# A DiT backbone's first modulation: 16 chunks row-major on TensorE, in four strips of the array's columns

## The chip, the core and the metric

The kernel runs as one program on one core of a Trainium2 chip. The metric is the device time of one execution in microseconds (us). Engines are named as the profile names them: PE is TensorE (PEld its weight loads), DVE is VectorE, ACT is ScalarE, POOL is GpSimd, SP is the engine that issues the DMAs.

## The reference

Two interleaved layers over 256 latent and 256 context tokens of width 1024: a macaron pair of SwiGLU FFNs (width 2816) around a gated short convolution (layer 0) or a latent attention (layer 1). Every sub-layer is normed and modulated by shift, scale and gate, which are linear maps of SiLU(c) for the latents and SiLU(c_ctx) for the context:

```python
def adaln_chunks(cond, w_mod, b_mod):
    m = jax.nn.silu(cond) @ w_mod + b_mod
    return jnp.split(m[:, None, :], N_MOD, axis=-1)

def pre(h, g, shift, scale):
    return rms_norm(h, g) * (1 + scale) + shift

def swiglu(h, w1, w3, w2):
    return (jax.nn.silu(h @ w1) * (h @ w3)) @ w2
...
        h_x = h_x + 0.5 * mx[2] * ffn1(pre(h_x, g_norm[i, 0], mx[0], mx[1]))
```

The first thing that the network needs is therefore `mx[0]`, `mx[1]` and their context twins for layer 0: shift (j = 0) and scale (j = 1), each of 1024 features, that is 8 chunks of 128 features each, 16 chunks in all.

## The kernel before

Activations are kept feature-major: `h` is 8 chunks of 128 features by 512 tokens (latents 0 to 255, context 256 to 511). Products are made in three matmuls (`mm3`, L167 to L169): weights and activations are split into a high part rounded to fp32r and a low rest, and high x high, low x high and high x low are added up in PSUM. Weights come as "units" of up to 128 x 2048 fp32 (1 MB), one DMA each into one of two `raw` buffers; `conv_unit` (L144, L145) makes the high part `wh` on ACT and the low part `wl` on DVE, in three buffers. A unit of the FFN's first product holds 8 blocks for w1 and 8 for w3, one block of 128 columns for each of the 8 contraction chunks.

The modulation is 144 chunks of 128 x 1024 (512 KB). `mod_order` sets their order; the first 16 are shift and scale of the first norm, taken in turn (shift 0, scale 0, shift 1, ...). Nearly all are stored transposed: a feature in each partition, and DVE multiplies them by the two condition rows `crow` and sums along the free axis (`mod_step`, L243, tile `junk`), two products a chunk; with `share`, the second product of a scale chunk goes to GpSimd (`pj`, L239) and ACT sums it (L240). Three of the first 16 are stored row-major (`_by_rows`): TensorE multiplies them by the 2 conditions as stationary columns (L226), ACT copies the 2 x 128 result (L230, tile `row`), TensorE transposes it (L232) and DVE adds the bias (L233). The finished values are in `fin`.

The opening, up to the end of the first three units of the first FFN, is written out as a list of steps, `FIRST_ORDER`, which `run` in `build` goes through: m and M compute one modulation chunk (M with `share`), w issues a chunk's DMA, r a unit's, U converts a unit, C0 to C7 is `chunk(k)`: the normed and modulated chunk k of the activations (`nt` on DVE or GpSimd, `nu` in two halves on ACT, `yh` on ACT, `yl` on DVE), S starts the FFN, T takes the third unit, A0 to A7 are the products of contraction chunk k with the first two units (12 matmuls), B0 to B7 those with the third (6). Z ends the time in which DMAs are issued by the list alone. A scheduler then places the instructions of each engine in order; each engine runs its own in that order. All weight and modulation DMAs are issued by SP, in order too. The first chunks' tiles lie in the FFN's still unused buffers `gh` and `gl` (`early`), the others in four buffers `wm`.

After the opening, the background modulation is paced by `bg`, some two to three chunks a step.

Of the kernel before, what the change touches and what calls it, by code (L numbers as in the profile page):

```python
# [9 lines left out]
F32 = mybir.dt.float32  # L10
F32R = mybir.dt.float32r
AF = mybir.ActivationFunctionType
ALU = mybir.AluOpType
AX = mybir.AxisListType

P = 128
D = 1024
ND = D // P
NLAT = 256
NCTX = 256  # L20
T = NLAT + NCTX
# [14 lines left out]
KR_N = KV_LORA + QK_ROPE  # L36
FIRST_ORDER = """m w w m C0 m U M U S M r A0 C1 w w m w M M w w U T B0 C2 A1 w m C3 M w m B1 B2 A2 B3 w M A3 C4 M B4 r C5 w A4 w M Z m C6 A5 B5 M A6 B6 C7 A7 r B7"""
MLA_ORDER = """L0 Q01 Q00 Q02 L1 R N0 n0 n1 T1 Q12 T0 Q10 n2 n3 Q11 N1 X1 n4 n5 D0 n6 n7 D1 D2 D3 D4 D5 D6 O0 D7 U K00 L2 L3 K10 T2 T3 V0 X3 K20 K30 O1 V1 V2 V3 H K31 K21 K11 K01"""
# [9 lines left out]
V_BMOD = 0  # L48
V_GN = V_BMOD + DEPTH * NMOD * ND
# [11 lines left out]
MODB = 4  # L61
EARLY = ("gh", "gl", None, "gh")
MOD_US = 8.0
WCOLS = 16 * P
# [4 lines left out]
class Kern:  # L69
# [17 lines left out]

    # ---------------------------------------------------------------- weights
    def plan(self):
# [69 lines left out]

    # ---------------------------------------------------------------- products  # L160
    def mm3(self, ps, c, u, b, x, k, start, stop):
# [20 lines left out]

    # ---------------------------------------------------------------- modulation
    def mod_setup(self):
        nc = self.nc
        self.mod = self.const.tile([P, DEPTH, NMOD * ND, 2], F32, name="mod")
        self.fin = self.const.tile([P, DEPTH, NMOD * ND, 2], F32, name="fin")
        self.mod_order = []
        for l in range(DEPTH):
            for js in ((0, 1), (2,), (3, 4), (5,), (6, 7), (8,)):  # L190
                for c in range(ND):
                    for j in js:
                        self.mod_order.append((l, j, c))
        self.mod_pos = 0
        self.mod_dma = 0
        self.mod_tiles = {}
        self.credit = 0.0
# [13 lines left out]

    def mod_step(self, share=False):
        if self.mod_pos >= len(self.mod_order):
            return
        nc = self.nc
        i = self.mod_pos
        self.mod_pos += 1
        l, j, c = self.mod_order[i]
        m = j * ND + c
        b = self.vec[:, V_BMOD + l * NMOD * ND + m:V_BMOD + l * NMOD * ND + m + 1]  # L220
        self.mod_dma_to(i + 1)
        w = self.mod_tiles.pop(i)
        if _by_rows(l, j, c):
            pr = self.mmps()
            for k in range(ND):
                nc.tensor.matmul(  # L226
                    pr[0:2, 0:P], self.cT[:, k, :], w[:, k * P:(k + 1) * P], start=k == 0, stop=k == ND - 1
                )
            row = self.gp.tile([2, P], F32, tag="row", name=self.nm("row"), bufs=2)
            nc.scalar.copy(row, pr[0:2, 0:P])  # L230
            pc = self.mmps()
            nc.tensor.transpose(pc[:, 0:2], row, self.ident[0:2, 0:2])  # L232
            nc.vector.tensor_scalar(self.fin[:, l, m, :], pc[:, 0:2], b, None, ALU.add)  # L233
            return
        for cond in range(2):
            o = self.mod[:, l, m, cond:cond + 1]
            if share and cond == 1 and j == 1:
                t = self.gp.tile([P, D], F32, tag="pj", name=self.nm("pj"), bufs=1)
                nc.gpsimd.tensor_tensor(t, w, self.crow[:, cond, :], ALU.mult)  # L239
                nc.scalar.activation(t, t, AF.Copy, accum_out=o)  # L240
                continue
            junk = self.gp.tile([P, D], F32, tag="junk", name=self.nm("junk"), bufs=1)
            ins = nc.vector.tensor_tensor_reduce(  # L243
                junk, w, self.crow[:, cond, :], 1.0, 0.0, ALU.mult, ALU.add, o
            )
            if share is False:
                self.tc.keep_in_program_order(ins)
        if not self.hold:
            self.mod_dma_to(i + 1 + MODB)
        src, dst = self.mod[:, l, m, :], self.fin[:, l, m, :]  # L250
        if j in (1, 4, 7):
            g = V_GN + (l * 3 + j // 3) * ND + c
            nc.vector.tensor_scalar(dst, src, b, 1.0, ALU.add, ALU.add)
            nc.vector.tensor_scalar(dst, dst, self.vec[:, g:g + 1], None, ALU.mult)
        elif j in (2, 8):
            nc.vector.tensor_scalar(dst, src, b, 0.5, ALU.add, ALU.mult)
        else:
            nc.vector.tensor_scalar(dst, src, b, None, ALU.add)  # L258

    def mod_need(self, l, js):  # L260
        need = max(i for i, (a, j, c) in enumerate(self.mod_order) if a == l and j in js)
        while self.mod_pos <= need:
            self.mod_step()
# [4 lines left out]
    def bg(self, us, quiet=False):  # L268
        """background modulation work, paced by the tensor engine's time"""
        self.credit += us  # L270
        n = 0
        while self.credit >= MOD_US and not quiet and n < 3:
            self.credit -= MOD_US
            self.mod_step()
            n += 1

    # ---------------------------------------------------------------- norms
    def rsqrt(self, ss, n, w, out):
# [63 lines left out]

    # ---------------------------------------------------------------- sublayer ends
    def residual(self, ps, d, c, l, j):
# [8 lines left out]
    def out_pair(self, u, x, ks, l, j, nxt, ctx_on):  # L353
        """last two chunks of a sub-layer's output, latents first, and the next norm"""
        nk = len(ks)
# [25 lines left out]
    def in_first(self, lat, ctx):  # L381
        """first groups of a sub-layer, contraction outermost, latents before the context"""
        for k in range(ND):
            for f in lat:
                f(k)
            if k == 1 and self.pending is not None:
                self.pending()
                self.pending = None
        for k in range(ND):
            for f in ctx:  # L390
                f(k)
# [3 lines left out]

    # ---------------------------------------------------------------- FFN
    def ffn_epi(self, p1, p3, g, f, w):
# [7 lines left out]
    def first_early(self, un, pss, g, l, j0):  # L405
        """first groups on unnormalized latents; the norm's factor is applied to their results"""
        nc = self.nc
# [100 lines left out]

    # ---------------------------------------------------------------- gated short convolution
    def conv_epi(self, pc, pu, pb, z, ch):  # L510
# [61 lines left out]

    # ---------------------------------------------------------------- latent attention
    def rot(self, src, tt, tabs, out, nh):
        """rotary halves of nh heads, token-major; gains are in the tables"""
        nc = self.nc
# [44 lines left out]
    def mla(self, l, nxt, mp):  # L621
        nc = self.nc
# [19 lines left out]

        # the rest of the last sub-layer's context; down projections, token-major
        held, g, ks, jg, sq = self.late
# [109 lines left out]

        # queries
        qps, qst = {}, {}
# [47 lines left out]

        # keys and values
        rctx = self.tmp.tile([P, T], F32, tag="rstd", name=self.nm("rstd"))[:, :NCTX]
# [85 lines left out]
        vv = []  # L892
        # heads, two at a time
        hp = QK_ROPE
# [106 lines left out]

    # ---------------------------------------------------------------- all
    def build(self):
# [19 lines left out]
        with self.tc.tile_pool(name="gp", bufs=1) as gp:  # L1023
            self.gp = gp
            self.mod_setup()
            for i in range(4):
                nc.sync.dma_start(self.h[:, 2 * i:2 * i + 2, :], a["hT"][:, 2 * i:2 * i + 2, :])
            self.mod_dma_to(2)
            self.dma_to(2)
            self.mod_dma_to(4)  # L1030
            self.crow = gp.tile([P, 2, D], F32, name="crow")
            nc.scalar.activation(self.cT, self.cT, AF.Silu)
            self.new_y()
# [36 lines left out]
            def run(ops, groups=None, more=None):  # L1070
                for op in ops:
                    k = int(op[1:] or 0)
                    if op[0] == "w":
                        self.mod_dma_to(self.mod_dma + 1)
                    elif op[0] == "r":
                        self.dma_to(self.dma_pos + 1)
                    elif op[0] == "M":
                        self.mod_step(True)
                    elif op[0] == "m":
                        self.mod_step(None)  # L1080
                    elif op[0] == "U":
# [34 lines left out]
def _by_rows(l, j, c):  # L1116
    """chunks of w_mod sent row-major, whose products go to the tensor engine"""
    return l == 0 and j == 0 and c < 3

# [86 lines left out]
```

## Time and profile before

| | |
|---|---|
| device time, median of 3 runs | 1659.9 us (1659.26 to 1659.95) |
| profiled execution: span, first to last instruction | 1657.4 us |
| what the runs' median has beside that span | 2.5 us |
| PE busy | 1614.2 us, 97% |
| DVE busy | 1156.7 us, 70% |
| ACT busy | 594.4 us, 36% |
| POOL busy | 94.3 us, 6% |
| DMA | 244.26 MB, mean 147 GB/s |
| granted TensorE clock, mean | 0.986 |

The profile has no separate device time of the profiled execution; its span stands in for it, and the runs' median is 2.5 us longer. A busy time is the time in which an engine has an instruction under way; matmuls overlap in it, so the distance between the starts of two matmuls, and not the duration of one, is what one costs. PEclk is the clock that the chip granted TensorE, as a share of full speed.

### The profile page before, as it was taken

How to read it: one execution, taken by the hardware profiler on the slowest of the kernel's cores; microseconds unless marked ns; L12 is line 12 of the kernel's file. 1: busy time of each engine (PE TensorE's matmuls, PEld its weight loads, DVE VectorE, ACT ScalarE, POOL GpSimd, SP SyncE). 2: the span in 40 equal slices, each digit the busy share in tenths (PEclk: the TensorE clock that was granted, in tenths of full speed). 3: DMA queues.
4: the chain of work that ended last, by engine and by line, in shares of the span. 5: the costliest groups of instructions: out<-in, count | busy, mean ns of one | idle time of the engine just before them, and what ended most of it. 6: DMA issues, size and time to landing. Idle time of an engine off the chain costs nothing.

```text
span 1657.4 us, 21462 instructions
## 1 busy us (share of the span) xinstructions
PE 1614.2 (97%) x8509; PEld 1380.1 (83%) x8509; DVE 1156.7 (70%) x2007; ACT 594.4 (36%) x936; POOL 94.3 (6%) x90
## 2 busy tenths in 40 slices
PE   6799999999999999999999999999999989999999
PEld 3588888888988898888888898888888976899999
DVE  7868667665897677766766677767664588786554
ACT  5342222323523253222232352222222466664442
POOL 3300000002000100000000200000000231010000
PEclk8899999999999999999999999999999979999999
DMA  7346445342254415444444425444432120146452
GB/s 306 135 148 221 154 140 195 141 157 102 81 212 170 172 52 194 162 165 152 167 164 165 140 77 186 157 162 156 165 140 102 58 77 1 67 163 216 167 202 102
DMA packets 46758, 244.26 MB, mean 147 GB/s; under 512 B 5313, under 2 KB 6593, under 8 KB 31041
## 3 DMA queue, kind: packets, MB, share of 16 engines
q1 hardware_dynamic: 46658, 242.90, 40.9%
q8 instruction: 66, 1.08, 0.3%
q14 instruction: 34, 0.28, 0.0%
HBM read 241.83 MB, written 1.05 MB: 147 GB/s over the span
## 4 chain that ended last, share of the span: by engine, by line
PE 90%; DVE 6%; DMA 2%; ACT 1%; issue 0%; POOL 0%; SPq 0%; DVEq 0%; ACTq 0%
PE mm L167 28%; PE mm L169 28%; PE mm L168 28%; DVE wl L145 1%; DVE junk L243 1%; DMA raw<-w 1%; DMA early<-wmod 1%; DVE yl L178 1%; PE mm L1045 0%; PE mm L942 0%; DVE nt L325 0%; PE mm L924 0%; PE mm L953 0%; DVE fin L258 0%; PE mm L687 0%
## 5 line engine op out<-in xcount | busy, mean ns | idle before, releaser
L167 PE MATMUL mm<-yh,wh 128*128 128x512 f32 (+1 forms) x1672 | 597.4, 358 | 6.2 <-ACT yh L177 4.1
L169 PE MATMUL mm<-yl,wh 128*128 128x512 f32 (+1 forms) x1672 | 595.3, 358 | 5.7 <-DVE yl L178 5.7
L168 PE MATMUL mm<-yh,wl 128*128 128x512 f32 (+1 forms) x1672 | 596.4, 357 | 0.8 <-DVE wl L145 0.8
L144 ACT CAST wh<-raw 128x1024 fp32r<-128x1024 f32 (+4 forms) x362 | 328.1, 931 | 618.6 <-PE mm L169 511.3
L145 DVE TENSOR_TENSOR wl<-raw,wh 128x1024 fp32r<-128x1024 f32 (+4 forms) x362 | 392.7, 1104 | 47.3 <-ACT wh L144 45.7
L167 PEld LDWEIGHTS mm<-yh,wh 128*128 128x128 f32 x1672 | 317.5, 190 | 53.1 <-ACT yh L177 4.9
L169 PEld LDWEIGHTS mm<-yl,wh 128*128 128x128 f32 x1672 | 317.0, 190 | 52.8 <-DVE yl L178 7.4
L168 PEld LDWEIGHTS mm<-yh,wl 128*128 128x128 f32 x1672 | 317.3, 190 | 46.2 <-DVE wl L145 1.5
L243 DVE CUSTOM_DVE_ANT_0 junk<-wm,crow 128x1024 f32<-128x1024 f32 x262 | 325.7, 1243 | 3.9
L167 PE MATMUL mm<-gh,wh 128*128 128x512 f32 (+1 forms) x848 | 294.9, 348 | 0.0
L169 PE MATMUL mm<-gl,wh 128*128 128x512 f32 (+1 forms) x848 | 294.4, 347 | 0.4 <-DVE gl L178 0.4
L168 PE MATMUL mm<-gh,wl 128*128 128x512 f32 (+1 forms) x848 | 294.2, 347 | 0.0
L402 DVE TENSOR_TENSOR s<-mm,s 128x512 f32<-128x512 f32 (+1 forms) x86 | 54.1, 629 | 246.7 <-PE mm L169 237.9
L169 PEld LDWEIGHTS mm<-gl,wh 128*128 128x128 f32 x848 | 160.5, 189 | 21.1 <-DVE gl L178 1.0
L349 DVE SCALAR_TENSOR_TENSOR h<-mm,fin,h 128x256 f32<-128x256 f32 x192 | 88.9, 479 | 127.7 <-PE mm L169 127.7
L168 PEld LDWEIGHTS mm<-gh,wl 128*128 128x128 f32 x848 | 160.5, 189 | 20.1
L167 PEld LDWEIGHTS mm<-gh,wh 128*128 128x128 f32 x848 | 160.5, 189 | 20.1
L401 ACT ACTIVATE s<-mm 128x512 f32<-128x512 f32 (+1 forms) x86 | 47.2, 548 | 193.4 <-PE mm L169 193.4
L178 DVE TENSOR_TENSOR gl<-s,gh 128x512 fp32r<-128x512 f32 (+1 forms) x86 | 53.5, 623 | 2.6 <-ACT gh L177 2.6
L297 POOL COPY acc<-sq 128x512 f32<-128x512 f32 (+1 forms) x5 | 4.4, 875 | 858.6 <-ACT sq L293 858.6
L293 ACT ACTIVATE sq<-h 128x256 f32<-128x256 f32 (+1 forms) x50 | 25.4, 508 | 72.9 <-DVE h L349 71.2
L177 ACT CAST gh<-s 128x512 fp32r<-128x512 f32 (+1 forms) x86 | 48.5, 564 | 4.4 <-DVE s L402 4.4
(187 smaller groups left out, 1064.0 us busy)
## 6 DMA issues: line engine op xcount, KB each, us to landing
raw<-w SPq DMA_DIRECT2D x104, 1024.0 KB, 4.8
wm<-wmod SPq DMA_DIRECT2D x132, 512.0 KB, 3.6
raw<-w SPq DMA_DIRECT2D x32, 896.0 KB, 4.5
raw<-cin_cu SPq DMA_DIRECT2D x8, 1024.0 KB, 4.9
early<-wmod SPq DMA_DIRECT2D x12, 512.0 KB, 10.4
raw<-cin_b SPq DMA_DIRECT2D x8, 512.0 KB, 3.8
raw<-cout SPq DMA_DIRECT2D x4, 1024.0 KB, 4.8
raw<-wo SPq DMA_DIRECT2D x4, 1024.0 KB, 4.8
```

The costliest lines, as they stand in the source:

```text
L144: self.nc.scalar.copy(h[:, b0:b1], raw[:, b0:b1])
L145: self.nc.vector.tensor_tensor(l[:, b0:b1], raw[:, b0:b1], h[:, b0:b1].bitcast(F32), ALU.subtract)
L167: mm(o, wh[:, b], xh[:, k, c[0]:c[1]], start=start, stop=False)
L168: mm(o, wl[:, b], xh[:, k, c[0]:c[1]], start=False, stop=False)
L169: mm(o, wh[:, b], xl[:, k, c[0]:c[1]], start=False, stop=stop)
L177: self.nc.scalar.copy(h, src)
L178: self.nc.vector.tensor_tensor(l, src, h.bitcast(F32), ALU.subtract)
L243: ins = nc.vector.tensor_tensor_reduce(junk, w, self.crow[:, cond, :], 1.0, 0.0, ALU.mult, ALU.add, o)
L293: nc.scalar.activation(sq[:, c[0]:c[1]], self.h[:, d, c[0]:c[1]], AF.Square)
L349: self.nc.vector.scalar_tensor_tensor(hh, ps[:, lo:hi], self.f(l, j, d, cond), hh, ALU.mult, ALU.add)
L401: nc.scalar.activation(s[:, :w], p1[:, :w], AF.Silu)
L402: nc.vector.tensor_tensor(s[:, :w], p3[:, :w], s[:, :w], ALU.mult)
```

## The change

All 16 chunks of the first modulation are now row-major (`_by_rows` is true for layer 0, j < 2), and `mod_rows` computes them in four groups G0 to G3 of four chunks: shift and scale of norm chunks 2g and 2g + 1. The conditions are padded with zeros to 32 columns (`cTp`). For each of 8 contraction chunks, four matmuls of 32 stationary columns on 128 moving ones go to four strips of 32 columns of the array, and their results to four strips of partitions of one PSUM tile. One copy of 128 x 128, one transpose and three DVE operations finish a group. `share` with its GpSimd and ACT path is gone, and `mod_pos` starts at 16. The list puts two norm chunks behind each group; four chunks of the second modulation (m) are done on DVE at the list's end. The DMAs of the first two groups are issued ahead: four chunks before the first two units, four behind them.

```diff
-FIRST_ORDER = """m w w m C0 m U M U S M r A0 C1 w w m w M M w w U T B0 C2 A1 w m C3 M w m B1 B2 A2 B3 w M A3 C4 M B4 r C5 w A4 w M Z m C6 A5 B5 M A6 B6 C7 A7 r B7"""
+FIRST_ORDER = """G0 U C0 C1 U S A0 A1 U T G1 C2 B0 B1 C3 A2 A3 B2 B3 G2 C4 A4 B4 C5 A5 B5 w w w w G3 Z C6 m A6 B6 C7 m A7 B7 m m"""
...
+NROW = 16
+CP = 32
...
-        self.mod_pos = 0
+        self.mod_pos = NROW
...
-        if _by_rows(l, j, c):
-            pr = self.mmps()
-            for k in range(ND):
-                nc.tensor.matmul(
-                    pr[0:2, 0:P], self.cT[:, k, :], w[:, k * P:(k + 1) * P], start=k == 0, stop=k == ND - 1
-                )
-            row = self.gp.tile([2, P], F32, tag="row", name=self.nm("row"), bufs=2)
-            nc.scalar.copy(row, pr[0:2, 0:P])
-            pc = self.mmps()
-            nc.tensor.transpose(pc[:, 0:2], row, self.ident[0:2, 0:2])
-            nc.vector.tensor_scalar(self.fin[:, l, m, :], pc[:, 0:2], b, None, ALU.add)
-            return
         for cond in range(2):
             o = self.mod[:, l, m, cond:cond + 1]
-            if share and cond == 1 and j == 1:
-                t = self.gp.tile([P, D], F32, tag="pj", name=self.nm("pj"), bufs=1)
-                nc.gpsimd.tensor_tensor(t, w, self.crow[:, cond, :], ALU.mult)
-                nc.scalar.activation(t, t, AF.Copy, accum_out=o)
-                continue
...
+    def mod_rows(self, g):
+
+        nc = self.nc
+        ws = [self.mod_tiles.pop(4 * g + q) for q in range(4)]
+        pr = self.mmps()
+        for k in range(ND):
+            for q, w in enumerate(ws):
+                nc.tensor.matmul(
+                    pr[q * CP:(q + 1) * CP, 0:P], self.cTp[:, k, :], w[:, k * P:(k + 1) * P],
+                    start=k == 0, stop=k == ND - 1, tile_position=(0, q * CP))
+        row = self.tmp.tile([P, T], F32, tag="t2", name=self.nm("row"), bufs=1)[:, 0:P]
+        nc.scalar.copy(row, pr[:, 0:P])
+        pc = self.mmps()
+        nc.tensor.transpose(pc[:, 0:P], row, self.ident)
+        src = pc[:, 0:P].rearrange("p (c j x) -> p c j x", c=2, j=2)
+        for j in range(2):
+            m = j * ND + 2 * g
+            v = lambda o: self.vec[:, o:o + 2].unsqueeze(2).broadcast_to([P, 2, 2])
+            dst = self.fin[:, 0, m:m + 2, :]
+            nc.vector.tensor_tensor(dst, src[:, :, j, 0:2], v(V_BMOD + m), ALU.add)
+            if j:
+                nc.vector.scalar_tensor_tensor(dst, dst, 1.0, v(V_GN + 2 * g), ALU.add, ALU.mult)
...
-            self.mod_dma_to(2)
+            self.mod_dma_to(4)
             self.dma_to(2)
-            self.mod_dma_to(4)
+            self.mod_dma_to(8)
             self.crow = gp.tile([P, 2, D], F32, name="crow")
-            nc.scalar.activation(self.cT, self.cT, AF.Silu)
+            self.cTp = gp.tile([P, ND, CP], F32, name="cTp")
+            nc.vector.memset(self.cTp, 0.0)
+            nc.scalar.activation(self.cTp[:, :, 0:2], self.cT, AF.Silu)
...
-                    if op[0] == "w":
+                    if op[0] == "G":
+                        if k < 2:
+                            self.dma_to(k + 3)
+                            self.mod_dma_to(4 * k + 12)
+                        self.mod_rows(k)
+                    elif op[0] == "w":
                         self.mod_dma_to(self.mod_dma + 1)
...
-                    elif op[0] == "M":
-                        self.mod_step(True)
...
-    return l == 0 and j == 0 and c < 3
+    return l == 0 and j < 2
```

How the scheduler places this shows at three places. First ScalarE, from the norm's factor on to the second unit's casts, before (`row` is the copy ahead of the transpose, `nu` a half of a norm chunk, `yh` its high part, `wh` a unit's high part):

```order
L230 COPY row_166<-mm_157 2x128
L144 CAST wh_201<-raw_99 128x512 x2
L1058 ACTIVATE nu_181<-nt_180,fin 128x256 x2
L144 CAST wh_218<-raw_101 128x512
L177 CAST yh_107<-nu_181 128x512
L144 CAST wh_218<-raw_101 128x512 x3
L230 COPY row_196<-mm_187 2x128
L240 ACTIVATE pj_213,mod<-pj_213 128x1024
```

and now:

```order
L255 COPY row_207<-mm_174 128x128
L1067 ACTIVATE nu_225<-nt_224,fin 128x256
L146 CAST wh_214<-raw_101 128x512 x4
L1067 ACTIVATE nu_225<-nt_224,fin 128x256
L1067 ACTIVATE nu_232<-nt_231,fin 128x256
L179 CAST yh_114<-nu_225 128x512
L1067 ACTIVATE nu_232<-nt_231,fin 128x256
L146 CAST wh_238<-raw_103 128x512
L179 CAST yh_114<-nu_232 128x512
```

The first unit's four casts and half of chunk 1 moved between the two halves of chunk 0 and its `yh`.

Second TensorE, around G1, now (`mm_253` is the last group of A1, `mm_297` the block's PSUM tile, `mm_288` the third unit's first group):

```order
L171 MATMUL mm_253<-yl_115,wh_238 128x512
L251 MATMUL mm_297<-early_105,cTp 32x128 x32
L257 MATMUL mm_332<-cst,row_330 128x128
L169 MATMUL mm_288<-yh_114,wh_278 128x512
L170 MATMUL mm_288<-yh_114,wl_279 128x512
L171 MATMUL mm_288<-yl_115,wh_278 128x512
```

Before, the three row-major chunks all stood ahead of the first product:

```order
L1047 MATMUL mm_109<-acc,ones 128x512
L226 MATMUL mm_157<-early_96,cT 2x128 x8
L232 MATMUL mm_168<-cst,row_166 128x2
L226 MATMUL mm_187<-early_96,cT 2x128 x8
L232 MATMUL mm_198<-cst,row_196 128x2
L226 MATMUL mm_234<-early_171,cT 2x128 x8
L232 MATMUL mm_245<-cst,row_243 128x2
L167 MATMUL mm_230<-yh_107,wh_201 128x512
```

Only G0 still does; G1 to G3 stand between products (three matmuls of G2 ahead of A2, its other 29 with all of G3 ahead of A4), the transposes of G1 and G2 directly behind their block, and that of G3 behind B5.

Third SP, the DMAs from the activations on, now (`early_96` is G0, `early_105` G1, `wm` of 166 to 172 G2, `early_292` G3, `raw` the units):

```order
L1034 DMA h<-hT 128x1024 x4
L210 DMA early_96<-wmod 128x1024 x4
L129 DMA raw_101<-w 128x2048
L129 DMA raw_103<-w 128x2048
L210 DMA early_105<-wmod 128x1024 x4
L129 DMA raw_164<-w 128x2048
L210 DMA wm_166<-wmod 128x1024
L210 DMA wm_168<-wmod 128x1024
L210 DMA wm_170<-wmod 128x1024
L210 DMA wm_172<-wmod 128x1024
L129 DMA raw_290<-w 128x2048
L210 DMA early_292<-wmod 128x1024 x4
```

Before, two chunks stood ahead of the first two units and four behind them; the third unit has G2 behind it now, and the fourth G3.

## Rows read from the trace of the kernel before

**Rows 1.** Page, part 2: the span in 40 slices of 41.4 us

```profile
PE   6799999999999999999999999999999989999999
...
PEclk8899999999999999999999999999999979999999
```

**Rows 2.** Windows: us, each engine's busy us (instructions), granted clock, DMA, GB/s

```profile
0.00:85.57 85.57, 59.48 (x205) 39.55 (x206) 69.49 (x99) 41.96 (x74) 29.44 (x20) 0.88 0.57 213
85.57:300.00 214.43, 214.43 (x947) 177.55 (x946) 152.12 (x249) 58.23 (x74) 0.00 (x0) 1.00 0.48 171
```

**Rows 3.** TensorE's waits up to 90 us: us, times, longest

```profile
PE mm L232 <- ACT row L230: 7.8, 3, 4.6
PE mm L169 <- DVE yl L178: 5.7, 3, 4.0
...
PE mm L167 <- ACT yh L177: 4.1, 2, 2.8
```

**Rows 4.** Timeline of TensorE: start, us, what, [idle before <-releaser]

```profile
16.63 2.82 PE L226 MATMUL mm<-early,cT 128*2 128x128 f32 x16
...
20.25 1.91 PE L226 MATMUL mm<-early,cT 128*2 128x128 f32 x16 [0.25 <-DMA early<-wmod]
...
25.13 3.40 PE L226 MATMUL mm<-early,cT 128*2 128x128 f32 x16
```

**Rows 5.** Timeline of ScalarE and VectorE, first norm chunk

```profile
19.48 0.25 ACT L230 COPY row<-mm 2x128 f32<-2x128 f32 x1 [0.31 <-PE mm L226]
...
20.25 0.21 DVE L233 TENSOR_SCALAR fin<-mm,vec 128x2 f32<-128x2 f32 x1
...
21.09 1.09 ACT L1058 ACTIVATE nu<-nt,fin 128x256 f32<-128x256 f32 x2 [0.32 <-DVE nt L1056]
...
22.60 0.61 ACT L177 CAST yh<-nu 128x512 fp32r<-128x512 f32 x1
...
34.16 2.17 ACT L144 CAST wh<-raw 128x512 fp32r<-128x512 f32 x4
```

**Rows 6.** Timeline of TensorE: pitch of its matmuls in the opening

```profile
33.34 0.80 PE L167 MATMUL mm<-yh,wh 128*128 128x512 f32 x1
...
38.63 0.80 PE L167 MATMUL mm<-yh,wh 128*128 128x512 f32 x2
...
75.66 0.50 PE L167 MATMUL mm<-yh,wh 128*128 128x512 f32 x1 [2.82 <-ACT yh L177]
...
80.11 0.39 PE L167 MATMUL mm<-yh,wh 128*128 128x512 f32 x1
...
85.57 0.39 PE L167 MATMUL mm<-yh,wh 128*128 128x512 f32 x1
```

**Rows 7.** Timeline of TensorE around a matmul on 64 rows, in the attention

```profile
1383.79 0.39 PE L923 MATMUL mm<-wh,arl 128*128 128x512 f32 x1
1384.11 0.50 PE L924 MATMUL mm<-wh,arh 64*128 64x512 f32 x1
1384.54 0.50 PE L922 MATMUL mm<-wl,arh 128*128 128x512 f32 x1
```

**Rows 8.** VectorE's and GpSimd's products up to 84 us; timeline at 36 us

```profile
L243 DVE CUSTOM_DVE_ANT_0 junk<-early,crow 128x1024 f32<-128x1024 f32 x14 | 19.2, 1374 | 0.0
...
L239 POOL TENSOR_TENSOR pj<-early,crow 128x1024 f32<-128x1024 f32 x4 | 11.4, 2860 | 0.4 <-ACT pj L240 0.4
...
35.91 2.82 POOL L239 TENSOR_TENSOR pj<-early,crow 128x1024 f32<-128x1024 f32 x1
...
36.42 2.34 DVE L253 TENSOR_SCALAR fin<-mod,vec 128x2 f32<-128x2 f32 x1
```

**Rows 9.** SP's issues; GB/s to 100 us, 40 slices of 2.5

```profile
10.19 1.94 SPq L208 DMA_DIRECT2D early<-wmod  x4
27.80 0.33 SPq L127 DMA_DIRECT2D raw<-w  x1
...
GB/s 6 224 379 367 408 428 426 410 398 48 0 79 410 418 419 411 426 380 359 48 0 41 216 162 16 210 324 288 0 0 0 0 0 0 7 216 256 367 69 298
```

More of the change, by code (lines that the diff above doesn't have):

```diff
@@ L210, in mod_dma_to, with mod_step @@
             self.mod_dma += 1
-    def mod_step(self, share=False):
+    def mod_step(self):
         if self.mod_pos >= len(self.mod_order):
@@ L245, in mod_step @@
             )
-            if share is False:
-                self.tc.keep_in_program_order(ins)
+            self.tc.keep_in_program_order(ins)
         if not self.hold:
@@ L1072, in run @@
                     k = int(op[1:] or 0)
-                    if op[0] == "w":
+                    if op[0] == "G":
[4 more added lines that the diff above has]
+                    elif op[0] == "w":
                         self.mod_dma_to(self.mod_dma + 1)
-                    elif op[0] == "r":
-                        self.dma_to(self.dma_pos + 1)
-                    elif op[0] == "M":
-                        self.mod_step(True)
                     elif op[0] == "m":
-                        self.mod_step(None)
+                        self.mod_step()
                     elif op[0] == "U":
```

## Prediction

> **What bounds the kernel now.** Read the page first: TensorE is busy in nine tenths or more of every slice but the first one or two and a few near the end, at full clock [rows 1]. So only a stretch where it waits can give time back. The windows place that stretch: up to 85.57 us TensorE is busy 59.48 us at a mean granted clock of 0.88, and from there to 300 us it is never idle [rows 2]. 85.57 us is where the fourth weight unit's first matmul starts. In this opening the 205 TensorE records are 8 for the condition rows, 2 for the norm's sum, 48 + 3 for the three row-major chunks and 144 for the three first weight units (8 contraction chunks, 6 groups, 3 products). At the pitch of the last 24, (85.57 - 80.11) / 24 = 0.2275 us [rows 6], the 144 need 32.8 us; they took 85.57 - 33.34 = 52.2. The opening's waits say for what: the transposed row (7.8 us), then yl and yh of the first norm [rows 3]. Behind these stand VectorE and GpSimd. VectorE's modulation products cost 19.2 us for 14 of its 20, GpSimd's 11.4 us for 4 of its 6; and while GpSimd multiplies (35.91 to 38.73), a VectorE fin of 128x2 elements lasts 2.34 us, where the like takes 0.21 [rows 8, 5]. So the reader should see a serial norm chain, held up by modulation work on two engines that stop each other. Order rows say that TensorE's sequence after the opening is the same in both kernels, so what is won or lost up to the fourth unit stays.
>
> **What the change takes away and adds.** It removes 20 VectorE products and 6 GpSimd ones for the first 16 chunks (20 x 1.37 = 27 and 6 x 2.86 = 17 us at the means of rows 8), which then no longer stand between the norm chunks. Four further chunks ("m", two products each) follow with the last norm chunks; I cost them at nothing, since they are taken from later work and VectorE is busy only 152 of 214 us after the opening [rows 2]; without that slack they would be 8 x 1.37, some 11 us. It adds four blocks G0 to G3 on TensorE, which did not exist: 32 matmuls each instead of 8, a copy of 128x128, a transpose and three small VectorE operations.
>
> *The price of a block.* Eight such matmuls with 2 stationary columns make 16 records, and took 2.82, 1.91 and 3.40 us [rows 4]: 1.91 at the clock's upper level (2.4 GHz; 0.119 us a record), 3.40 at the lower (1.2). No row shows four strips of columns at work together. If nothing overlaps a block is 4 x 1.91 = 7.6 us; if the four overlap fully, 1.9. I take 3.8, the middle that one mechanism gives: each matmul is two records in the same strip, which follow each other, and if starts stay in order only one record of a strip can run beside one of the next, so a block is 32 x 0.119 = 3.8. The Trainium skill, "TensorE: Matmul & The Clock Gate" (Part 3), has matmuls in strict order and a measured 2.38-fold gain for three column tiles; by that a block would be an estimated 3.2 us and the time 1653.
>
> *Up to the first product.* G0 starts where the first block started, 16.63 us [rows 4]: its chunks no longer queue behind two weight units (10.19 us issue, landed at 20.2 before; 2.1 MB less ahead of them at some 410 KB a us is 5 us earlier) [rows 9, 4]. It ends at 20.4. Copy to fin took 19.48 to 20.46 with one VectorE operation [rows 5]; with three, and waits, 1.6: 22.0. Then ScalarE, in the order above: half of nu, the first unit's four casts (2.17), two halves (0.55 each, 1.09 for two), yh 0.61 [rows 5]: 0.55 + 2.17 + 1.09 + 0.61 = 4.4, so 26.5 with handoffs. Before it was 33.34: 6.8 us earlier.
>
> *From there on TensorE is nearly the bound.* 144 x 0.2275 = 32.8. Low clock after the wait of some 5 us: before, the 12 matmuls from 33.34 to 38.63 took 5.3 instead of 2.7 [rows 6], so 2.6 once more; it hides the second unit's casts. G1 to G3 lie between products in TensorE's order: 3 x 3.8 = 11.4. Behind G1 and G2 TensorE's next instruction is the transpose, which waits for the copy: 0.7 each, 1.4. Norm chunks 2 to 5 are then finished behind 12 to 36 queued matmuls (2.7 to 8.2 us against a chain of 3.5), so they cost nothing; were a block faster, they would show first at chunk 2. Chunk 6 has no such cover: G3's transpose stands behind all products of chunks 4 and 5, so fin, three halves and yh follow it: 0.3 + 0.7 + 1.6 + 0.6 = 3.2 idle, and a slower clock after it as after the 2.82 us wait at 75.66, where 12 matmuls took 4.45 instead of 2.73 [rows 6]: 1.7. Entering and leaving the tiled form: the 64-row matmul in the attention starts 0.32 after the one before and the next 0.43 after it, where 0.2275 is usual [rows 7], so some 0.2 a switch with what trails; ten switches, half of them inside waits: 1.0. The Trainium skill, "TensorEngine Tiling (Array Packing)" (Key Properties), says that a change of tiling mode drains the engine; rows 7 agree, at that small price, so the rule speaks against this change by 1 us and not by more.
>
> Sum: 26.5 + 32.8 + 2.6 + 11.4 + 1.4 + 3.2 + 1.7 + 1.0 = 80.6 against 85.57: 5.0 us. The profiled span of 1657.4 becomes 1652.4. The median of the runs shown, 1659.9, stands 2.5 above that span, so the forecast is **1655**.
>
> *Queues.* On SP the third unit's transfer (issued at 27.80 us before [rows 9]) waits for the first unit's conversion, now with G2's four chunks behind it, and the fourth unit's for the second's, with G3's behind that. The first conversion ends near 26.5, so 1.05 + 2.1 MB land by some 36 us and the next 3.1 MB by 45; TensorE wants G2 at 42 and G3 at 55 by the terms above. That cover of 6 to 10 us is the reason for costing both queues at nothing. GpSimd keeps its seven norm multiplications alone; each can hold VectorE about 1.3 us, and yl is behind yh, where two to four products need no yl.
>
> **Rivals.**
> *Strips one after another.* The four strips are only an arrangement, and records go one by one. For it: none of the kernel's rows has two matmuls at once in different strips. Against: weight loads of 128 columns, 177.55 us for 946 [rows 2], already hide behind running matmuls. The Trainium skill, "TensorE: Matmul & The Clock Gate" (Part 3), also says that weight loads overlap running matmuls only in other row groups, which all four strips share; rows 2 contradict it for full-width loads. Price: 3.8 more in each of four blocks, 15.2: opening ends near 96, 10 us later than before, time 1670. It decides from a block of 3.8 + 5.0 / 4 = 5.1 us on; there the change gains nothing.
> *Full overlap.* A block of 1.9 us: 7.6 less, 1647 to 1648. The norm chain then shows at chunks 2 and 4 and gives some of it back: 1650.
> *Low clock inside the blocks.* The third block before ran at 3.40 instead of 1.91 [rows 4]. If the clock falls in G2 and G3, which follow each other, or stays low behind G0, a block is up to 1.8 times as long and the products behind it lose 1.7 to 2.6: 3 to 10 us, time 1658 to 1665. The same range holds strips that overlap by a third only.
>
> **How the numbers follow.** Half overlap as forecast, with blocks of 3 to 4.3 us: 1652 to 1658, chance 0.50. Nearer full overlap: 1647 to 1652, 0.15. Low clock or weak overlap: 1658 to 1667, 0.20. No overlap: 1667 to 1674, 0.15. A measurement of this kernel tells about 0.2%, 3.3 us, from no change, so faster begins below 1656.6: 0.35 of the first case and the second, 0.50. Same, to 1663.2: 0.15 and 0.12, 0.27. Slower: 0.08 and 0.15, 0.23. The range leaves out no overlap and a little below: 1648 to 1667; the likeliest case's own is 1652 to 1658.
>
> **What would show it.** First product of the first unit at 26 to 27 us; G blocks of 32 matmuls in 3 to 4.3 us each, with start distances of 0.05 to 0.07 us a record; no custom product on VectorE before 60 us and none on GpSimd; one idle of about 3 us ahead of chunk 6; first matmul of the fourth unit at 80 to 81 us; from there the same as before. Wrong if records of a block stand 0.11 us or more apart, if TensorE waits for a transfer of G2 or G3 or for unit 3's conversion, or if the time moves outside the opening.

## The result and the profile after

| | before | after |
|---|---|---|
| median of the runs | 1659.6 us | 1648.55 us |
| ratio, 95% interval | | 0.9932, 0.9918 to 0.9946 |
| profiled span | 1657.4 us | 1647.3 us |
| fourth unit's first matmul | 85.57 us | 75.94 us |
| from there to the span's end | 1571.8 us | 1571.4 us |

The change made the kernel 11.0 us faster by the medians, 10.1 by the two spans. 9.6 of the 10.1 lie ahead of the fourth unit and 0.5 behind it: the rest of the kernel is unmoved, as forecast. The times are medians, here of four runs each; of the experiments below, one run of e1 took 5107 us and is left out. The forecast was 1655 us with a range from 1648 to 1667; the time lies 0.6 us inside the range's lower end, in the case that was called full overlap and had a chance of 0.15.

The page of the changed kernel, part 2, the span in 40 slices of 41.2 us (for [rows 1]):

```profile
PE   6999999999999999999999999999999979999999
```

Windows of the changed kernel, cut at the fourth unit's first matmul; the columns are those of [rows 2]:

```profile
0.00:75.94 75.94, 56.69 (x414) 40.06 (x415) 35.48 (x61) 35.05 (x63) 11.16 (x14) 0.91 0.67 255
75.94:290.40 214.46, 214.41 (x946) 177.19 (x945) 148.95 (x241) 58.55 (x74) 0.00 (x0) 1.00 0.47 168
```

TensorE has 414 records in the opening in place of 205, and still fewer busy us; VectorE's busy time is halved (69.49 to 35.48) and GpSimd's falls from 29.44 to 11.16. TensorE's waits up to 90 us (us, times, longest; for [rows 3]):

```profile
PE mm L169 <- ACT yh L179: 8.9, 3, 5.4
...
PE mm L257 <- ACT row L255: 2.3, 3, 1.5
```

The waits for yl are gone. What is left are three waits for yh and the three for a block's row. The same on TensorE's timeline (start, us, what, idle before; for [rows 4, 6]): L251 are the blocks' matmuls, L257 the transposes, L169 a product's first matmul.

```profile
15.21 2.08 PE L1056 MATMUL mm<-acc,ones 128*128 128x512 f32 x2 [5.49 <-DVE acc L1050]
17.21 2.56 PE L251 MATMUL mm<-early,cTp 128*32 128x128 f32 x64
21.32 0.33 PE L257 MATMUL mm<-cst,row 128*128 128x128 f32 x1 [1.54 <-ACT row L255]
27.03 0.79 PE L169 MATMUL mm<-yh,wh 128*128 128x512 f32 x1 [5.39 <-ACT yh L179]
...
35.30 1.95 PE L251 MATMUL mm<-early,cTp 128*32 128x128 f32 x64
...
49.39 1.94 PE L251 MATMUL mm<-wm,cTp 128*32 128x128 f32 x58
51.68 0.33 PE L257 MATMUL mm<-cst,row 128*128 128x128 f32 x1 [0.36 <-ACT row L255]
51.94 1.95 PE L251 MATMUL mm<-early,cTp 128*32 128x128 f32 x64
54.72 0.50 PE L169 MATMUL mm<-yh,wh 128*128 128x512 f32 x1 [0.82 <-ACT yh L179]
...
63.08 0.27 PE L257 MATMUL mm<-cst,row 128*128 128x128 f32 x1
66.05 0.61 PE L169 MATMUL mm<-yh,wh 128*128 128x512 f32 x1 [2.70 <-ACT yh L179]
...
70.50 0.40 PE L169 MATMUL mm<-yh,wh 128*128 128x512 f32 x1
...
75.94 0.61 PE L169 MATMUL mm<-yh,wh 128*128 128x512 f32 x2
76.61 0.50 PE L170 MATMUL mm<-yh,wl 128*128 128x512 f32 x1
```

G2's first three matmuls (six records) stand at 40.65 us, between products. A block of 32 matmuls in four strips lasts 1.95 us, as long as a block of 8 did before [rows 4]. The chain ahead of the first product, on ScalarE, VectorE and GpSimd in that order (for [rows 5]):

```profile
21.00 0.27 ACT L255 COPY row<-mm 128x128 f32<-128x128 f32 x1 [2.26 <-DVE rstd L295]
22.80 0.60 ACT L1067 ACTIVATE nu<-nt,fin 128x256 f32<-128x256 f32 x1 [1.54 <-DVE fin L265]
23.31 2.16 ACT L146 CAST wh<-raw 128x512 fp32r<-128x512 f32 x4
```

```profile
21.94 0.83 DVE L265 SCALAR_TENSOR_TENSOR fin<-fin,vec 128x4 f32<-128x4 f32 x1
```

```profile
21.05 1.70 POOL L1065 TENSOR_TENSOR nt<-h,rstd 128x512 f32<-128x512 f32 x1 [16.05 <-DMA raw<-w]
```

The copy waits for rstd, which it doesn't read: the row shares a buffer (tag t2) with an intermediate of the norm's rsqrt, which the operation that makes rstd reads last. And a fin of 128x4 elements takes 0.83 us beside GpSimd's multiplication.

### The profile page after: what moved, and what is told of

Same layout as the page of the kernel before. It is cut to its first block, busy times and chain, and to the rows that moved or that the text cites. A ratio compares the mean times of both kernels' runs of the same rounds, so it can differ in the third digit from the quotient of the medians.

```text
span 1647.3 us, 21814 instructions
## 1 busy us (share of the span) xinstructions
PE 1609.7 (98%) x8718; PEld 1378.9 (84%) x8718; DVE 1117.1 (68%) x1956; ACT 587.2 (36%) x925; POOL 75.9 (5%) x84
## 4 chain that ended last, share of the span: by engine, by line
PE 93%; DVE 3%; ACT 2%; issue 0%; POOL 0%; DMA 0%; SPq 0%; DVEq 0%; ACTq 0%
PE mm L169 29%; PE mm L171 29%; PE mm L170 29%; PE mm L949 0%; DVE junk L228 0%; PE mm L931 0%; DVE nt L332 0%; PE mm L960 0%; DMA h<-hT 0%; ACT wh L146 0%; PE mm L694 0%; POOL tr L593 0%; PE mm L961 0%; PE mm L251 0%; DVE rstd L295 0%
## 5 line engine op out<-in xcount | busy, mean ns | idle before, releaser
L169 PE MATMUL mm<-yh,wh 128*128 128x512 f32 (+1 forms) x1672 | 597.0, 358 | 11.0 <-ACT yh L179 8.9
L147 DVE TENSOR_TENSOR wl<-raw,wh 128x1024 fp32r<-128x1024 f32 (+4 forms) x362 | 388.0, 1092 | 48.8 <-ACT wh L146 46.9
L169 PEld LDWEIGHTS mm<-yh,wh 128*128 128x128 f32 x1672 | 316.9, 190 | 57.6 <-ACT yh L179 9.7
L228 DVE CUSTOM_DVE_ANT_0 junk<-wm,crow 128x1024 f32<-128x1024 f32 x256 | 315.8, 1234 | 4.0
L169 PE MATMUL mm<-gh,wh 128*128 128x512 f32 (+1 forms) x848 | 294.9, 348 | 0.0
L169 PEld LDWEIGHTS mm<-gh,wh 128*128 128x128 f32 x848 | 160.5, 189 | 20.2
L306 POOL TENSOR_TENSOR acc<-acc,sq 128x512 f32<-128x512 f32 (+1 forms) x36 | 42.2, 1173 | 117.2 <-ACT sq L300 117.1
```

The source lines that it names most:

```text
L147: self.nc.vector.tensor_tensor(l[:, b0:b1], raw[:, b0:b1], h[:, b0:b1].bitcast(F32), ALU.subtract)
L169: mm(o, wh[:, b], xh[:, k, c[0]:c[1]], start=start, stop=False)
L228: ins = nc.vector.tensor_tensor_reduce(junk, w, self.crow[:, cond, :], 1.0, 0.0, ALU.mult, ALU.add, o)
L306: nc.gpsimd.tensor_tensor(self.acc[:, c[0]:c[1]], self.acc[:, c[0]:c[1]], sq[:, c[0]:c[1]], ALU.add)
```

## Experiments

All edits are to the changed kernel, but for the one on the kernel before. Ratios are to the kernel before, measured on the same chip. The readings from traces are of one execution each. In these the first block starts anywhere from 16.50 to 17.81 us, before an edit can act, and the stretch from the first product to the second block, which begins at a low clock, takes 7.6 to 8.5 us where nothing in it waits. So where times of two runs are compared closely, they are counted from the first or the second block's start.

### Do the strips run side by side?

**e1_strip_after_strip**, the same 32 matmuls, strip by strip:

```diff
-        for k in range(ND):
-            for q, w in enumerate(ws):
+        for q, w in enumerate(ws):
+            for k in range(ND):
```

> The 32 matmuls of a block in another order: all eight of one strip, then the next strip; nothing else is changed. Theory (records of neighbouring strips run side by side, records of one strip go one after another): a block takes four times the 1.91 us of rows 4, about 7.6 us, in place of 1.95; G1 to G3 bring 3 x 5.7 = 17 us, G0 5.7 us on the path to the first product, so the fourth unit's first matmul moves from 75.9 to some 94 to 99 us and the time from 1648.5 to 1667 to 1672, slower than the kernel before. Rival (a matmul into 32 columns with 128 moving columns is short by itself, whatever stands next to it): blocks stay at 1.95 us and the time at 1648.5.

Measured: 1663.1 us, ratio 1.002 (1.0011 to 1.003). A block of this run, on TensorE's timeline:

```profile
62.98 5.96 PE L251 MATMUL mm<-early,cTp 128*32 128x128 f32 x64
```

**e2_two_strips**, two strips alternate, then the other two:

```diff
-        for k in range(ND):
-            for q, w in enumerate(ws):
+        for k, q, w in ((k, q, ws[q]) for h in (0, 2) for k in range(ND) for q in (h, h + 1)):
```

> Two strips alternate, then the other two; nothing else is changed. Theory (records run side by side as far as strips alternate): a block takes half of four times 1.91, about 3.8 us, G1 to G3 and G0 bring 4 x 1.85 = 7.4 us at most, the time is 1653 to 1656. Rival one (a single pair record runs beside the next, so two strips already give all there is): 1.95 us and 1648.5. Rival two (only strips far apart overlap): near 7.6 us and 1667.

Measured: 1652.8 us, ratio 0.9959 (0.9945 to 0.9972):

```profile
35.86 3.29 PE L250 MATMUL mm<-early,cTp 128*32 128x128 f32 x64
```

The order of the matmuls alone moves a block from 5.96 through 3.29 to 1.95 us, so it is the alternation of strips that makes them overlap, and the rival of matmuls that are short by themselves falls. With a record's own 0.27 us taken off the end, the starts are 5.69 / 63 = 0.090, 0.048 and 0.027 us apart: 1.9-fold for two strips and 3.4-fold for four (1.8 and 3.05 by the whole blocks). The sizes of both expectations were off: four blocks of 8 matmuls with two columns (4 x 1.91) overstate 32 serial ones with 32 columns. Without overlap the change is 0.2% slower than the kernel before; the packing is what makes it pay.

### Where the blocks stand

**e3_g3_early**, the fourth block right behind the third:

```diff
-... B3 G2 C4 A4 B4 C5 A5 B5 w w w w G3 Z C6 ...
+... B3 G2 G3 C4 A4 B4 C5 A5 B5 w w w w Z C6 ...
```

> The fourth block is put right behind the third in the order, ahead of the products of chunks 4 and 5. Theory (TensorE's 2.70 us idle ahead of chunk 6 is there only because the fourth transpose stands behind those products, and the slow clock after it follows from that idle): the idle at 66.05 goes to under 0.3 us and the nine matmuls behind it take 2.0 in place of 3.75 us, so the fourth unit's first matmul moves from 75.9 to some 71.5 us, and the time from 1648.5 to 1644 to 1645. Rival one (chunk 6 is late for another reason: its norm multiplication on GpSimd, the third unit's conversion or a transfer): an idle of 1 to 3 us stays, time 1646 to 1648.5. Rival two (TensorE then reaches the fourth unit before its weights are there): the gain comes back as a wait at the fourth unit, time 1648.

Measured: 1644.85 us, ratio 0.9911 (0.9898 to 0.9925), 3.7 us under the changed kernel. The idle ahead of chunk 6 is gone, the clock stays at its upper level (1.00 granted from 55.08 to 71.81 us), and the fourth unit comes at 71.81. Its second matmul then waits:

```profile
71.81 0.39 PE L169 MATMUL mm<-yh,wh 128*128 128x512 f32 x1
73.00 0.50 PE L170 MATMUL mm<-yh,wl 128*128 128x512 f32 x1 [0.80 <-DVE wl L147]
```

So the place of one block cost about 4 us, the expected size, and 0.8 came back in the place of the second rival: VectorE makes its eight late products without a pause from 59.98 to 70.96 us, and the fourth unit's wl stands behind them. In the changed kernel these products begin at 66.64, so e3 moved VectorE's queue along with the idle; the last section shows that this queue, and not the slow clock, set the time there.

**e6_g3_no_late_products**, as e3, with these products left to the background work of the later stages:

```diff
-... Z C6 m A6 B6 C7 m A7 B7 m m
+... Z C6 A6 B6 C7 A7 B7
```

> The fourth block behind the third, and the four chunks with two VectorE products each, which the change put with the last norm chunks, are taken out of the opening; the background work of the later stages then makes them. Theory (with TensorE ahead, these eight products, some 10 us in a row on VectorE, stand ahead of the fourth unit's wl and make its 0.80 us wait): the wait goes, the fourth unit's products run through, time 1643.9 to 1644.1. Rival (the products are missed later, where they come at a worse place): the wait goes, but the rest of the kernel takes 1 to 8 us longer, time 1645 to 1652.

Measured: 1644.8 us, ratio 0.9915 (0.9902 to 0.9929). The wait is gone, and the time is that of e3: by the spans the stretch behind the fourth unit's first matmul is 0.6 us longer (1643.6 - 72.11 against 1642.7 - 71.81), though it holds no wait of 0.8. The products may cost about as much later; that isn't shown, since the intervals can't tell the 0.6 from nothing.

**e4_c0_first**, the first norm chunk ahead of the first conversion:

```diff
-G0 U C0 C1 U S ...
+G0 C0 U C1 U S ...
```

> The first norm chunk is put ahead of the first unit's conversion in the order; on ScalarE both halves of nu and yh then stand ahead of three of the four casts. Theory (the first product, at 27.03 us, is held by the casts that stand between the halves of nu): it comes at 25.0 to 25.5 us, and as TensorE is nearly the bound from there, the time falls by 1 to 1.9 us, to 1646.6 to 1647.5. Rival (the first products are then held by the remaining casts, yl or the second unit's transfer): the first product is earlier, but waits of the same length stand behind it, and the time stays within 0.5 us of 1648.5.

Measured: 1649.5 us, ratio 0.9944 (0.9931 to 0.9958): no gain, although the first product is at 24.26. TensorE's timeline shows where it went:

```profile
16.50 3.12 PE L251 MATMUL mm<-early,cTp 128*32 128x128 f32 x64
...
24.26 0.79 PE L169 MATMUL mm<-yh,wh 128*128 128x512 f32 x1 [3.33 <-ACT yh L179]
...
36.93 0.50 PE L170 MATMUL mm<-yh,wl 128*128 128x512 f32 x1 [0.45 <-DVE wl L147]
...
48.46 1.94 PE L251 MATMUL mm<-wm,cTp 128*32 128x128 f32 x60
...
62.27 0.43 PE L251 MATMUL mm<-early,cTp 128*32 128x128 f32 x8
66.11 0.50 PE L169 MATMUL mm<-yh,wh 128*128 128x512 f32 x1 [2.70 <-ACT yh L179]
```

Counted from the first block's start, e4 is 2.1 us ahead of the changed kernel at the first product (7.8 against 9.8) and 0.2 at the third block (32.0 against 32.2): the early start went, as the rival had it, into waits for casts and wl of the first two units (the largest is shown). At chunk 6 it is 0.8 behind (49.6 against 48.8), since eight records of the fourth block came to stand behind the products.

**e5_g3_c0**, both edits:

> Both reorderings at once: the fourth block behind the third, and the first norm chunk ahead of the first unit's conversion. In the run with the first norm chunk ahead alone, the third block began 0.9 us earlier than in the changed kernel, and this was lost where the fourth block's last strip stood behind the products of chunks 4 and 5. Theory (that loss was the split fourth block and nothing else): with the fourth block early the 0.9 us come on top, the fourth unit's first matmul at 70.9 in place of 71.8, time 1643.9 against 1644.85; where the wait for wl at the fourth unit takes it, 1644.8. Rival (the earlier start is lost in waits for casts and wl of the first two units whatever follows): 1644.9 to 1646.

Measured: 1646.1 us, ratio 0.9923 (0.9909 to 0.9936): the rival. The 0.9 us of the expectation was read off the times of two executions, and 0.7 of it was the first block's earlier start in e4. The block isn't split here, and the gain is gone all the same. Counted from the first block's start, the 25th product matmul comes 20.0 us later (20.3 in e3), the 37th 24.0 (23.6): waits of 0.23, 0.19 and 0.43 us for wl and wh stand ahead of these.

**e9_g2_early**, the third block one step earlier:

```diff
-... A2 A3 B2 B3 G2 C4 A4 B4 C5 A5 B5 w w w w G3 Z C6 ...
+... A2 A3 G2 B2 B3 G3 C4 A4 B4 C5 A5 B5 w w w w Z C6 ...
```

> The third block is put ahead of chunk 2 and 3's second groups, the fourth behind them. Theory (the 0.82 us ahead of chunk 4's first product and the 0.36 ahead of the third transpose are there since only the fourth block stands between the third block and chunk 4): both go, the fourth unit's first matmul comes about 1.1 us earlier than with the fourth block early alone, but VectorE's eight late products then hold the fourth unit's wl as long as before in absolute terms minus what they start earlier: time 1643.7 to 1644.9. Rival (the third block's chunks have not landed yet at that place): a wait for a transfer in front of the block, 1645 to 1648.

Measured: 1643.5 us, ratio 0.9905 (0.9888 to 0.9921). The 0.82 ahead of chunk 4 and the 0.36 ahead of the third transpose are gone, and 0.41 is left of the wait for wl. From the second block's start to the fourth unit it takes 34.8 us in place of 36.1 in e3, so the theory's 1.1 is there; the two ratios' intervals overlap.

### VectorE and GpSimd

**e7_before_no_pool**, the kernel before, where VectorE makes the six products that GpSimd made:

```diff
-                        self.mod_step(True)
+                        self.mod_step(None)
```

> The kernel before, with the six GpSimd products of the opening made by VectorE instead. Theory of the prediction (VectorE and GpSimd stop each other, so that a GpSimd product costs VectorE about as much as making it itself): VectorE gets 6 x 1.37 = 8.2 us more and loses as much in stalls; the time stays within 2 us of the kernel before. Rival (the GpSimd products run beside VectorE and take load off it): the opening grows by most of the 8.2 us, time 1664 to 1668. Other rival (they were pure harm): 1650 to 1655.

Measured: 1652.3 us, ratio 0.9959 (0.9946 to 0.9973): the other rival, pure harm, 6.7 us by the medians. The fourth unit's first matmul comes at 78.10 in place of 85.57. The window up to there, with the columns of [rows 2]:

```profile
0.00:78.10 78.10, 55.61 (x206) 35.59 (x206) 63.48 (x111) 35.22 (x61) 15.07 (x14) 0.96 0.61 234
```

About half of these 7.5 us is TensorE's clock: it is busy 55.61 us in place of 59.48, at a granted clock of 0.96 in place of 0.88; the rest is waits. The profiled execution is the fastest of this kernel's four. VectorE's costliest groups up to there (busy us, mean ns), of this run and then of the kernel before:

```profile
L243 DVE CUSTOM_DVE_ANT_0 junk<-early,crow 128x1024 f32<-128x1024 f32 x18 | 23.0, 1276 | 0.1
...
L243 DVE CUSTOM_DVE_ANT_0 junk<-wm,crow 128x1024 f32<-128x1024 f32 x8 | 9.7, 1216 | 0.0
...
L258 DVE TENSOR_SCALAR fin<-mod,vec 128x2 f32<-128x2 f32 x5 | 1.1, 225 | 0.1
```

```profile
L243 DVE CUSTOM_DVE_ANT_0 junk<-wm,crow 128x1024 f32<-128x1024 f32 x6 | 9.5, 1583 | 0.0
L258 DVE TENSOR_SCALAR fin<-mod,vec 128x2 f32<-128x2 f32 x5 | 5.3, 1068 | 0.1
```

Six products more cost VectorE 4.0 us (32.7 for 26 against 28.7 for 20 [rows 8]), and its busy time in the opening falls from 69.49 to 63.48 us. The Trainium skill, "SBUF — State Buffer" (Who interferes with whom), says that VectorE and GpSimd share a pair of ports that one of them holds for a whole instruction; these rows agree, and [rows 8] most plainly: the fin there ends at 38.76 us, the GpSimd product beside it at 38.73.

The edit also takes ScalarE's six sums of the GpSimd products away (L240), and one of them stood ahead of a yh for which TensorE waited 1.26 us in the kernel before:

```profile
61.26 1.04 ACT L240 ACTIVATE pj<-pj 128x1024 f32<-128x1024 f32 x1
...
62.30 0.60 ACT L177 CAST yh<-nu 128x512 fp32r<-128x512 f32 x1
```

So VectorE's 6.0 us are shown; how the gain divides between the stalls, these sums and the longer way from GpSimd over ScalarE to fin, the run doesn't tell.

**e8_g3_norm_on_vector**, as e3, with the norm multiplications on VectorE:

```diff
-                (nc.gpsimd if k else nc.vector).tensor_tensor(t, self.h[:, k, :], r, ALU.mult)
+                nc.vector.tensor_tensor(t, self.h[:, k, :], r, ALU.mult)
```

> The fourth block behind the third, and the seven norm multiplications of the opening that GpSimd made are made by VectorE too. Theory (in the opening GpSimd's multiplications stretch VectorE's operations beside them: fin 0.16 to 0.83 or 1.0 us, yl 0.69 to 1.11, wl 0.69 to 1.76, some 3 us in all, of which 0.7 stand in the chain to the first product): seven multiplications of 0.69 us come to VectorE, those stretches go, the first product is 0.3 to 0.7 us earlier, time 1644 to 1644.9. Rival (VectorE's queue then holds fin or yl back): chunks wait longer, 1645.5 to 1648.

Measured: 1642.6 us, ratio 0.99 (0.9885 to 0.9915): by the median more than the theory's size, though the interval overlaps that of e3. The fin of 0.83 us is one of 0.16:

```profile
22.08 0.16 DVE L265 SCALAR_TENSOR_TENSOR fin<-fin,vec 128x4 f32<-128x4 f32 x1
```

ScalarE's casts moved too: in this run they start right behind the row copy, at 20.83, and the first product is at 25.05, 8.2 us behind the first block's start in place of 9.8 in e3. How much of the gain is the order and how much the stalls, this run doesn't tell.

### The best version

**e10_g2_norm_on_vector** is e9 with e8's edit; **e11_g2_norm_own_row** also gives the row its own buffer:

```diff
-        row = self.tmp.tile([P, T], F32, tag="t2", name=self.nm("row"), bufs=1)[:, 0:P]
+        row = self.gp.tile([P, P], F32, tag="row", name=self.nm("row"), bufs=1)
```

> The two edits that each took time off, together: third and fourth block earlier, the seven norm multiplications on VectorE. Theory (they act at different places, the one on the waits ahead of the third transpose and chunk 4, the other on the chain to the first product and on VectorE's late operations): 1.1 us off the 1642.6 of the norm multiplications on VectorE with the fourth block early, time 1641.3 to 1641.8. Rival (the eight late products of VectorE, which start no earlier, hold the fourth unit's wl): 1642.3 to 1643.

> As the run before it, and the row that holds a block's result gets a buffer of its own, in place of the one it shares with the rsqrt of the norm. Theory (the first block's row copy waits for rstd only through the shared buffer, and ScalarE's casts stand behind it): the copy comes 0.4 to 0.8 us earlier and the first product 0.4 us, time 0.3 to 0.5 us under the run before it. Rival (the casts then wait for the first unit's transfer, and fin stands behind the norm multiplications anyway): no difference.

Measured: 1641.4 us, ratio 0.9893 (0.9876 to 0.9909), and 1640.2 us, ratio 0.9886 (0.9871 to 0.9901). e10 came as expected, and from the second block's start to the fourth unit it takes 34.8 us in place of 35.9 in e8. In e11 the copy waits for the block alone:

```profile
19.94 0.27 ACT L255 COPY row<-mm 128x128 f32<-128x128 f32 x1 [1.89 <-PE mm L251]
```

Counted from the first block's start the first product comes at 7.8 us (8.2 in e8 and e10), as the theory had it; that the medians of e10 and e11 lie 1.2 apart, the intervals don't confirm. e11 is 8 us faster than the changed kernel and 19 us faster than the kernel before.

## Why the prediction was right, and what it mis-sized

The range held, by 0.6 us, and so did the way and the place of the gain; the likeliest case, 1652 to 1658, did not come, and the gain of 5 us became one of 11. The prediction's terms beside what the changed kernel's rows give, in us:

| term | forecast | after |
|---|---|---|
| first product | 26.5 | 27.03 |
| 144 matmuls | 32.8 | 32.6 (pitch (75.94 - 70.50) / 24) |
| low clock behind the first wait | 2.6 | 2.7 |
| G1 to G3 | 11.4 | 6.2 |
| waits of two transposes | 1.4 | 0.75 |
| idle ahead of chunk 4 | named, not in the sum | 0.82 |
| idle ahead of chunk 6 | 3.2 | 2.70 |
| slow clock behind it | 1.7 | 1.7 in 12 matmuls, hidden behind VectorE |
| eight late products | 0 | set the fourth unit's first wl product, at 76.61 |
| mode switches | 1.0 | 1.4, what is left, with the transposes themselves |
| fourth unit | 80.6 | 75.94 |

**The price of a block** is the term that was mis-sized: 3.8 us in the sum, 1.95 in the trace. It failed twice in one direction. The serial price was taken from blocks of 16 records with two columns, 7.6 us for four, where e1 shows 5.96; and "only one record of a strip can run beside one of the next" is refuted by the changed kernel: it allows the 1.8-fold that two strips give in e2, but no more than 2-fold, and four strips give 5.96 / 1.95 = 3.05-fold. The Trainium skill, "TensorE: Matmul & The Clock Gate" (Part 3), has 2.38-fold for three column tiles; two and four stand on either side of it here.

The 1.95 is near the 1.9 of the full-overlap rival, and not for its reason: a quarter of e1's 5.96 would be 1.5.

**The first product** came out near by luck: two errors cancel. The forecast had the block, the copy and fin in a row. The first block took 2.56 in place of 3.8 us, but the row copy waited until 21.00 for rstd through the shared buffer, which the order of instructions didn't show and a reading of the buffers' tags would have. So the block's length didn't count: in e3 it was 3.64 us, and the first product still came 9.8 us behind the block's start, as in the changed kernel. e11 undoes that wait.

**The idle ahead of chunk 6** was forecast by place, cause and size; e3 shows the cause. The slow clock behind it came in its size too, but it isn't a sure consequence of the idle and cost no time of its own (last section). The prediction said that a block faster than forecast would show first at chunk 2. No wait is there; it showed at chunk 4, which has only the fourth block between the third transpose and its products.

**"Two engines that stop each other"** was right, and worth more than the prediction made of it: e7 moves only the six GpSimd products to VectorE, with ScalarE's sums of them gone, and that alone brings 7.5 of the 9.6 us ahead of the fourth unit, or 6.7 of 11.0 by the medians. The prediction spoke of the removed products as one thing.

**"I cost them at nothing"**, said of the eight late products, is the step whose reason failed. It looked at VectorE's slack behind the opening, and not at its queue ahead of the fourth unit's wl. In the changed kernel that wl ends at 76.56 us and the first matmul that reads it starts at 76.61, some 0.2 us later than TensorE's pitch alone would have it; where TensorE was ahead, in e3, the products made a wait of 0.80, and in e1 and e2 one of 1.61.

**The rivals.** Strips one after another would have been slower, as said, by 0.2% and not by 10 us (e1). The time of full overlap is what came; its give-back was 0.82, at chunk 4 alone. The clock did not fall inside G1 to G3: 1.00 granted in each.

**Queues.** No wait for G2's or G3's transfer shows; that cover held.

**A reading.** [rows 1] has one slice near the end below nine tenths, not a few; nothing rests on it.

## What to carry to other kernels

Small matmuls with few output columns pay on TensorE when the inner loop walks the strips, so that neighbours in the order stand in different strips; walked strip by strip, the same instructions took three times as long. Before a product is given to GpSimd to relieve VectorE, compare VectorE's mean durations with and without it: here the help cost 7 us. Where a block with a transpose feeds the next chunk, put it a few products earlier than its use, and look at which tags its buffers share. Before work on another engine is costed at nothing, follow that engine's queue to the next thing that TensorE needs from it.

## What the runs showed that was not expected

The same idle had two outcomes for the clock. In the changed kernel and in e2, TensorE waits 2.70 us ahead of chunk 6, behind 36 matmuls at the upper level and one transpose. The windows behind it (us, TensorE's busy us, granted clock, DMA, GB/s), of the changed kernel and of e2, 12 matmuls each:

```profile
66.05:70.50 4.45, 4.45 (x13) 0.62 0.00 0
```

```profile
69.70:72.40 2.70, 2.70 (x12) 1.00 0.00 0
```

At 0.62 the stretch lies mostly at the lower of the clock's levels (1.2 GHz), at 1.00 all of it at the upper (2.4 GHz); the 12 matmuls take 1.7 us longer. Behind the same wait e1 shows 1.00 as well, and e4, with the eight late records of the fourth block ahead of the transpose, 0.62. In the two kernels whose clock fell TensorE had also waited ahead of chunk 4 (0.82 and 1.04 us), in the two others it had not. That is one execution of each, and e2's four runs differ in mean granted clock (0.990 to 0.994), so chance isn't ruled out; what decides it was not tried.

The slow clock cost no time of its own. The first matmul that reads the fourth unit's wl, in e2:

```profile
80.26 0.50 PE L170 MATMUL mm<-yh,wl 128*128 128x512 f32 x1 [1.61 <-DVE wl L147]
```

From chunk 6's first matmul to the first one that reads the fourth unit's wl it is 80.26 - 69.70 = 10.56 us here, at the upper clock, and 76.61 - 66.05 = 10.56 in the changed kernel, at 0.62; e1 and e4 have 10.56 as well. VectorE sets it: from chunk 6's yl to that wl it works without a pause, with six of the eight late products in between. What the clock gave back, TensorE waited for wl. So a term for the slow clock behind an idle of this length should stand in a range with zero in it, and beside it the other engines' queues up to the next unit.
